# Where a matmul's moving columns come from: one run of memory, or two places in turn

## The chip, the cores and the metric

The kernel runs on one core of a Trainium2 chip. A core has a matmul engine (PE, with its weight loads shown apart as PEld), a vector engine (DVE), a scalar engine (ACT), GpSimd (POOL) and a queue engine that issues most DMAs (SP). Operands lie in an on-chip memory of 128 partitions; matmuls write to a second one, PSUM, from which DVE and ACT read. The metric is the device time of one execution in microseconds (us), the median of several runs.

A matmul has two operands. The *stationary* one, 128 x 128, is loaded into the array by a weight load (LDWEIGHTS); the *moving* one, 128 partitions x 256 or 512 columns, is then streamed through it column by column. Here most operands are of the type fp32r: four bytes a value, rounded, done in one pass. A plain fp32 matmul is done in two.

## The reference

One layer of a trunk with three branches, for 256 tokens of width 2048. All weights are fp32.

```python
h = rms_norm(x, pre_g)
proj = h @ w_in                                  # 2048 -> 7*1024 + 3*2048
a_u, a_v, a_g, b_x, b_g, x_q, x_g, gate_logits = jnp.split(proj, splits, axis=-1)
y_a = spatial_gating(a_u, a_v, sg_ln_g, sg_ln_b, sg_w, sg_b) * jax.nn.silu(a_g)
y_b = s5_branch(b_x, ..., glu_w, glu_b) * jax.nn.silu(b_g)
y_x = memory_cross_attention(x_q, rms_norm(mem, mem_g), xa_wk, xa_wv) * jax.nn.silu(x_g)
branch = jnp.einsum('bsnc,ncd->bsnd', jnp.stack([y_a, y_b, y_x], axis=2), w_branch)
gates = jax.nn.sigmoid(gate_logits.reshape(bsz, seq, N_BRANCH, D_MODEL))
out = jnp.sum(gates * branch, axis=2) @ w_out
return x + rms_norm(out, post_g)
```

The attention reads 256 memory tokens; `s5_branch` is a scan over the 256 positions with a product with `glu_w` behind it.

## The kernel before

**Two halves of every number.** To come close to fp32 with one-pass matmuls, each weight and each activation is split into a high part, rounded to fp32r by ACT, and a low part, the rest, made by DVE (`split`, `split_to`, lines 93 and 94). A product is then high x high + low x high + high x low.

**Two kinds of product.** `cm` products put out channels on the partitions and tokens along the columns: a 128 x 128 block of weights is stationary and the activations move. `cm_mm` does a step over 128 input channels in two matmuls: the high weights against the high and low halves of the activations side by side (512 columns, line 132), and the low weights against the high half (256 columns, line 131, or 134 in the first step). The two sums that stand apart in PSUM are added by `fold` or `fold_u`. `tm` products put out tokens on the partitions: a block of activations is stationary and 512 columns of weights move; `tm_mm` does a step in three matmuls of 512 columns (lines 137 to 139). The normalised x lies in `xhl`, 16 tiles `x` of 128 channels x (high, low) x 256 tokens; the memory tokens lie alike in four tiles `H`, as `mhl`.

**Weights** come from HBM in pieces of 1 MB (`load`, tiles `raw`, three buffers), and are split in halves of 1024 columns into tiles `hl` (three buffers). The host lays them out beforehand (`layouts`: `cm`, `tm`).

**Stages, in PE's order.** The first half of the S5 input (`start`, with x arriving alongside), the rest of it (`w_bx`), queries (`w_xq`), keys (`wk`) and values (`wv`) of the memory, the attention's gate (`w_xg`), then `merge` for the attention branch (`w_gate`, `w_br`), the gating branch (`w_av`, `w_ag`, `w_au`), its merge, the S5 gate (`w_bg`) and its merge with the product by `glu`, and the output (`w_out`, and `w_out3` in two blocks of 256 columns).

**What sets the order.** PE's instructions stand in the order in which the code writes them. Small work (the S5 scan `s5_main`, attention, layer norm, transposes) is made of generators that `pump` advances between the blocks, a few steps at a time, by credits. Splits of weights are issued ahead of it. DVE, ACT and POOL take their instructions in the scheduler's order.

**Names that the change touches.** `norm_split` writes x and the memory tokens as high and low parts. `bc` is the row of 1/rms by token. `s5_prep` splits a block of `u` (the S5 input, later its output) into `uhl` and copies pieces of it to `U4`, which moves in `bu_mm` (line 511). `s5_gelu` works on `u` in place; its split goes to `yg` in the tiles `H2` and `H3`. `evac_k` takes the keys out of PSUM into `kT` (a tile `M`). `attn` uses pieces of the queries `qT` as stationary (line 661) and transposes the weights of attention `p`; `attn_out` writes the attention's output; `sg_z` multiplies by `zT`. `yB` is the S5 branch's output, stationary in the last branch product.

Of the kernel before, what the change touches and what calls it, by code (L numbers as in the profile page):

```python
# [18 lines left out]
P = 128  # L19
# [25 lines left out]
def trunk(ctx: ExitStack, tc: tile.TileContext, I, out):  # L45
# [74 lines left out]

    def norm_split(src, gv, dst, k0):
        for k in range(len(dst)):
            kk = k0 + k
            r = src[:, k * T:(k + 1) * T]
            a.activation(out=dst[k][:, 0], in_=r, func=AF.Copy, scale=gv[:, kk:kk + 1])
            v.scalar_tensor_tensor(out=dst[k][:, 1], in0=r, scalar=gv[:, kk:kk + 1],
                                   in1=dst[k][:, 0].bitcast(F32), op0=ALU.mult, op1=ALU.subtract)

    def cm_mm(ps, wh, wl, hl, first, last):
        if not first:  # L130
            pe.matmul(ps[:, 0:T], lhsT=wl, rhs=hl[:, 0], start=False, stop=False)  # L131
        pe.matmul(ps, lhsT=wh, rhs=hl.rearrange("p h t -> p (h t)"), start=first, stop=last)  # L132
        if first:
            pe.matmul(ps[:, 0:T], lhsT=wl, rhs=hl[:, 0], start=False, stop=False)  # L134

    def tm_mm(ps, wh, wl, hl, ts_, first, last):
        pe.matmul(ps, lhsT=hl[:, 0, ts_], rhs=wh, start=first, stop=False)  # L137
        pe.matmul(ps, lhsT=hl[:, 0, ts_], rhs=wl, start=False, stop=False)  # L138
        pe.matmul(ps, lhsT=hl[:, 1, ts_], rhs=wh, start=False, stop=last)  # L139
# [27 lines left out]
    def cm_block(ps, raw, hl):  # L167
        for hf in range(2):
            wh, wl = split(raw[:, hf * 1024:(hf + 1) * 1024], CM_OFF)
            for k in range(8):  # L170
                kk = hf * 8 + k
                cm_mm(ps, wh[:, k * P:(k + 1) * P], wl[:, k * P:(k + 1) * P], hl[kk], kk == 0, kk == 15)
            pump(rate["cm"])

    def tm_quarter(acc, raw, hl, kq, nk):
        for hf in range(2):
            wh, wl = split(raw[:, hf * 1024:(hf + 1) * 1024])
            for k in range(2):
                kk = kq * 4 + hf * 2 + k
                sl = slice(k * 512, (k + 1) * 512)  # L180
                for tb in range(2):
                    tm_mm(acc[tb], wh[:, sl], wl[:, sl], hl[kk], slice(tb * P, (tb + 1) * P), kk == 0, kk == nk - 1)
# [8 lines left out]
    def cm_pairs(src, nblk, hl, evac):  # L191
        for bp in range(nblk // 2):
            ps = acc_tile()
            for b in range(2):
                cm_block(ps[:, b], load(src[2 * bp + b]), hl)
# [8 lines left out]
    xhl = [xp.tile([P, 2, T], F32R, name=f"x{k}") for k in range(16)]  # L204
# [40 lines left out]
    def rms_row(key, sss, targets):  # L245
# [24 lines left out]
        a.copy(out=bc[:, 0, :], in_=ps[:, 0:T])  # L270
# [13 lines left out]
    mh = [slot(f"H{i}", [P, 4, 2, T], F32R) for i in range(4)]  # L284
    mhl = [mh[k // 4][:, k % 4] for k in range(16)]
# [180 lines left out]
    def s5_load(q):  # L466
        rw = s5p.tile([P, 2, P], F32, tag="rw", name=nm("sb"))
        if q < 2:
            g.tensor_copy(out=rw[:, 0, 0:1], in_=mhl[0][:, 0, 0:1].bitcast(F32))
# [3 lines left out]
    def s5_prep(q, rw, hl):  # L473
# [601 lines left out]
```

## Time and profile before

| | |
|---|---|
| median of 3 runs | 964.48 us (964.4 to 964.81) |
| profiled execution | 964.42 us |
| its span, first to last instruction | 962.7 us |
| DMA engines' mean rate | 201 GB/s |
| weight loads on PE | 4864 |

The profile is one execution. *Busy* is the time in which an engine had an instruction running; for PE the end of a matmul is modelled, and neighbours overlap, so its busy share says that matmuls stood behind each other, not how fast they went. The groups (one line of code, one engine, one shape) give count, busy time, mean duration and idle time before. The order of time gives the start of each instruction. The stage rows give, for a stretch of the span, each engine's busy time, the granted clock of PE and the DMAs' share.

### The profile page before, as it was taken

How to read it: one execution, taken by the hardware profiler on the slowest of the kernel's cores; microseconds unless marked ns; L12 is line 12 of the kernel's file. 1: busy time of each engine (PE TensorE's matmuls, PEld its weight loads, DVE VectorE, ACT ScalarE, POOL GpSimd, SP SyncE). 2: the span in 40 equal slices, each digit the busy share in tenths (PEclk: the TensorE clock that was granted, in tenths of full speed). 3: DMA queues.
4: the chain of work that ended last, by engine and by line, in shares of the span. 5: the costliest groups of instructions: out<-in, count | busy, mean ns of one | idle time of the engine just before them, and what ended most of it. 6: DMA issues, size and time to landing. Idle time of an engine off the chain costs nothing.

```text
span 962.7 us, 13036 instructions
## 1 busy us (share of the span) xinstructions
PE 949.8 (99%) x4864; PEld 799.7 (83%) x4864; DVE 781.2 (81%) x1382; ACT 544.5 (57%) x892; POOL 23.9 (2%) x46
## 2 busy tenths in 40 slices
PE   9999999999999999999999999999999999999996
PEld 7878888888888878888888888888887878888886
DVE  6889759965769989999777799999998966775555
ACT  7555756655456657564544566566656546544442
POOL 1100000000000001000000000000000000000000
PEclk9999999999999999999999999999999999999999
DMA  9757855545355556555555545556555555557542
GB/s 358 257 219 264 303 182 186 212 156 206 131 188 178 207 203 221 201 187 206 181 189 182 203 170 197 186 189 222 180 186 189 196 198 204 182 184 268 198 175 88
DMA packets 30464, 193.34 MB, mean 201 GB/s; under 512 B 3904, under 2 KB 4416, under 8 KB 8640
## 3 DMA queue, kind: packets, MB, share of 16 engines
q1 hardware_dynamic: 28288, 186.18, 54.0%
q0 software_dynamic: 1536, 4.20, 1.2%
q10 hardware_dynamic: 576, 2.12, 0.7%
q8 instruction: 38, 0.62, 0.3%
q14 instruction: 26, 0.21, 0.1%
HBM read 190.39 MB, written 2.10 MB: 200 GB/s over the span
## 4 chain that ended last, share of the span: by engine, by line
PE 88%; DVE 8%; ACT 1%; issue 1%; DMA 1%; POOL 0%; SPq 0%; DVEq 0%; ACTq 0%
PE acc L132 19%; PE acc L137 18%; PE acc L138 18%; PE acc L139 18%; PE acc L131 9%; DVE hl L94 3%; DVE p L323 1%; PE y L576 1%; PE po L692 1%; PE bu L511 1%; ACT hl L93 1%; DMA sb<-s5b 1%; PE acc L134 1%; PE sc L661 1%; DVE p L552 1%
## 5 line engine op out<-in xcount | busy, mean ns | idle before, releaser
L94 DVE TENSOR_TENSOR hl<-raw,hl 128x1024 fp32r<-128x1024 f32 x319 | 388.9, 1219 | 138.6 <-ACT hl L93 137.2
L93 ACT CAST hl<-raw 128x1024 fp32r<-128x1024 f32 x319 | 334.6, 1049 | 269.8 <-PE acc L139 153.2
L132 PE MATMUL acc<-x,hl 128*128 128x512 f32 x736 | 255.6, 393 | 0.5 <-ACT hl L93 0.5
L131 PE MATMUL acc<-x,hl 128*128 128x256 f32 x690 | 194.7, 282 | 1.4 <-DVE hl L94 1.3
L137 PE MATMUL acc<-hl,x 128*128 128x512 f32 x448 | 176.2, 393 | 0.0
L138 PE MATMUL acc<-hl,x 128*128 128x512 f32 x448 | 174.7, 390 | 0.0
L139 PE MATMUL acc<-hl,x 128*128 128x512 f32 x448 | 174.3, 389 | 0.0
L132 PEld LDWEIGHTS acc<-x,hl 128*128 128x128 f32 x736 | 135.9, 188 | 28.2 <-ACT hl L93 1.0
L131 PEld LDWEIGHTS acc<-x,hl 128*128 128x128 f32 x690 | 129.9, 188 | 5.0 <-DVE hl L94 3.0
L137 PEld LDWEIGHTS acc<-hl,x 128*128 128x128 f32 x448 | 84.1, 188 | 18.8 <-issue 2.1
L139 PEld LDWEIGHTS acc<-hl,x 128*128 128x128 f32 x448 | 84.1, 188 | 17.8
L138 PEld LDWEIGHTS acc<-hl,x 128*128 128x128 f32 x448 | 84.2, 188 | 16.6
L137 PE MATMUL acc<-hl,H 128*128 128x512 f32 (+1 forms) x224 | 85.9, 384 | 0.0
L138 PE MATMUL acc<-hl,H 128*128 128x512 f32 (+1 forms) x224 | 85.6, 382 | 0.0
L139 PE MATMUL acc<-hl,H 128*128 128x512 f32 (+1 forms) x224 | 85.5, 382 | 0.0
L132 PE MATMUL acc<-H,hl 128*128 128x512 f32 x192 | 66.4, 394 | 0.3 <-DVE H L94 0.3
L131 PE MATMUL acc<-H,hl 128*128 128x256 f32 x176 | 49.4, 280 | 0.8 <-ACT H L93 0.8
L139 PEld LDWEIGHTS acc<-hl,H 128*128 128x128 f32 x224 | 42.1, 188 | 8.3
L499 ACT ACTIVATE t<-E,pwr 128x32 f32<-128x32 f32 (+2 forms) x96 | 33.9, 354 | 26.6 <-DVE E L326 25.5
L137 PEld LDWEIGHTS acc<-hl,H 128*128 128x128 f32 x224 | 42.1, 188 | 8.2 <-issue 0.4
L138 PEld LDWEIGHTS acc<-hl,H 128*128 128x128 f32 x224 | 42.1, 188 | 7.7
L323 DVE TENSOR_TENSOR p<-p,E 128x512 f32<-128x512 f32 x64 | 44.0, 687 | 0.9
(243 smaller groups left out, 1180.6 us busy)
## 6 DMA issues: line engine op xcount, KB each, us to landing
raw<-w_gate SPq DMA_DIRECT2D x48, 1024.0 KB, 4.7
raw<-w_br SPq DMA_DIRECT2D x24, 1024.0 KB, 4.7
raw<-w_out SPq DMA_DIRECT2D x16, 1024.0 KB, 4.7
raw<-w_xq SPq DMA_DIRECT2D x8, 1024.0 KB, 4.8
raw<-wk SPq DMA_DIRECT2D x8, 1024.0 KB, 4.8
raw<-wv SPq DMA_DIRECT2D x8, 1024.0 KB, 4.9
raw<-w_xg SPq DMA_DIRECT2D x8, 1024.0 KB, 4.7
raw<-w_av SPq DMA_DIRECT2D x8, 1024.0 KB, 4.8
```

The costliest lines, as they stand in the source:

```text
L93: a.copy(out=hi, in_=src)
L94: v.tensor_tensor(out=lo, in0=src, in1=hi.bitcast(F32), op=ALU.subtract)
L131: pe.matmul(ps[:, 0:T], lhsT=wl, rhs=hl[:, 0], start=False, stop=False)
L132: pe.matmul(ps, lhsT=wh, rhs=hl.rearrange("p h t -> p (h t)"), start=first, stop=last)
L134: pe.matmul(ps[:, 0:T], lhsT=wl, rhs=hl[:, 0], start=False, stop=False)
L137: pe.matmul(ps, lhsT=hl[:, 0, ts_], rhs=wh, start=first, stop=False)
L138: pe.matmul(ps, lhsT=hl[:, 0, ts_], rhs=wl, start=False, stop=False)
L139: pe.matmul(ps, lhsT=hl[:, 1, ts_], rhs=wh, start=False, stop=last)
L323: v.tensor_tensor(out=o, in0=i0, in1=i1, op=op)
L499: a.activation(out=t, in_=E[:, :, lo_], func=AF.Copy, scale=ci)
L511: pe.matmul(bu[:, ri, :], lhsT=B4[:, ri, :], rhs=U4, start=True, stop=True)
L552: v.tensor_tensor_scan(out=p2[:, ri], data0=rb, data1=p1[:, ri], initial=0.0, op0=ALU.mult, op1=ALU.add)
```

## The change

Every fp32r matmul takes the columns of its moving operand in turn from two places: first place, second place, first place again one column on. `two` writes that as an access pattern. For a 512-column operand the places are 1 KB apart (256 values); for the 256-column weights of `w_out3` and for `U4` they are half of that.

The data is laid out so that this gives what it gave before:

- The host stores each 512-column block of `tm` weights (and each 256-column block of `w_out3`) with its even columns first and its odd ones behind; taking turns puts them in order again.
- A tile of x or of the memory tokens is now (token half, high or low, 128 tokens), so that tokens b and 128 + b are 1 KB apart (`Pairs`). A `cm` product then puts out its columns as tokens 0, 128, 1, 129 and so on.
- Whatever reads such columns undoes it or keeps to it: `in_order` and `in_order2` read or write them with a step of two (the row of 1/rms, gelu, the attention's output, the gating product), `qT` and `p` give their pieces as every second column, `yB` gives its stationary pieces as every second column (`Plain` with `turn`), and the S5 split undoes two turns at once with a step of four.

Two further edits: the key products use `cm_mm3`, three matmuls of 256 columns that add into one place in PSUM, so that `evac_k` only copies; and the split of the gelu output goes in eight pieces of 256 in place of four of 512.

```diff
+    def two(z):
+        return z.rearrange("p (a b) -> p b a", a=2)
+    def in_order(z):
+        return z.rearrange("p (b c) -> p c b", c=2)
...
+    class Pairs:
...
+        def half(self, h):
+            return self.t[:, :, h]
+        def moving(self, h):
+            return self.t[:, :, h].rearrange("p c b -> p b c")
+        def moving_both(self):
+            return two(self.t.rearrange("p c h b -> p (c h b)"))
+        def stationary(self, h, tb):
+            return self.t[:, tb, h]
+    class Plain:
...
+        def stationary(self, h, tb):
+            return self.t[:, h, tb::2] if self.turn else self.t[:, h, tb * P:(tb + 1) * P]
...
     def cm_mm(ps, wh, wl, hl, first, last):
         if not first:
-            pe.matmul(ps[:, 0:T], lhsT=wl, rhs=hl[:, 0], start=False, stop=False)
-        pe.matmul(ps, lhsT=wh, rhs=hl.rearrange("p h t -> p (h t)"), start=first, stop=last)
+            pe.matmul(ps[:, 0:T], lhsT=wl, rhs=hl.moving(0), start=False, stop=False)
+        pe.matmul(ps, lhsT=wh, rhs=hl.moving_both(), start=first, stop=last)
...
+    def cm_mm3(ps, wh, wl, hl, first, last):
+        pe.matmul(ps[:, 0:T], lhsT=wh, rhs=hl.moving(0), start=first, stop=False)
+        pe.matmul(ps[:, 0:T], lhsT=wh, rhs=hl.moving(1), start=False, stop=False)
+        pe.matmul(ps[:, 0:T], lhsT=wl, rhs=hl.moving(0), start=False, stop=last)
+
+    def tm_mm(ps, wh, wl, hl, tb, first, last):
+        pe.matmul(ps, lhsT=hl.stationary(0, tb), rhs=two(wh), start=first, stop=False)
+        pe.matmul(ps, lhsT=hl.stationary(0, tb), rhs=two(wl), start=False, stop=False)
+        pe.matmul(ps, lhsT=hl.stationary(1, tb), rhs=two(wh), start=False, stop=last)
...
-    xhl = [xp.tile([P, 2, T], F32R, name=f"x{k}") for k in range(16)]
+    xhl = [Pairs(xp.tile([P, 2, 2, P], F32R, name=f"x{k}")) for k in range(16)]
...
-            split_to(hl[:, 0], hl[:, 1], u[:, q // 4, :])
+            split_to(*(hl[:, z].rearrange("p (a c b) -> p a c b", a=2, c=2) for z in range(2)),
+                     u[:, q // 4, :].rearrange("p (b a c) -> p a c b", a=2, c=2))
...
-            pe.matmul(bu[:, ri, :], lhsT=B4[:, ri, :], rhs=U4, start=True, stop=True)
+            pe.matmul(bu[:, ri, :], lhsT=B4[:, ri, :], rhs=two(U4), start=True, stop=True)
...
-        for k in range(4):
-            d = yg[k // 2][:, 2 * (k % 2):2 * (k % 2) + 2]
-            split_to(d[:, :, 0], d[:, :, 1], u[:, 2 * k:2 * k + 2, :])
-            yield 0.7
...
+        for k in range(8):
+            d = nrm["yg"][k]
+            split_to(d.half(0), d.half(1), in_order(u[:, k, :]))
+            yield 0.35
...
     def s5_gelu(cb, ps):
-        y = u[:, cb, :]
-        stt(y, y, d_s5[:, cb:cb + 1], ps, ALU.mult, ALU.add)
+        y = in_order(u[:, cb, :])
+        stt(y, y, d_s5[:, cb:cb + 1], ps.rearrange("p (c b) -> p c b", c=2), ALU.mult, ALU.add)
...
     def evac_k(bp, ps):
-        fold_u(kT[:, 2 * bp:2 * bp + 2, :], ps)
+        a.copy(out=kT[:, 2 * bp:2 * bp + 2, :], in_=ps[:, :, 0:T])
...
-    cm_pairs(I["wk"], 8, mhl, evac_k)
+    cm_pairs(I["wk"], 8, mhl, evac_k, cm_mm3)
...
-                pe.matmul(sc[:, qb, :], lhsT=qT[:, 2 * h + c, qb * P:(qb + 1) * P], rhs=kT[:, 2 * h + c, :],
+                pe.matmul(sc[:, qb, :], lhsT=qT[:, 2 * h + c, qb::2], rhs=kT[:, 2 * h + c, :],
...
-        return np.ascontiguousarray(w.reshape(kq, 4, 128, nn, 512).transpose(3, 0, 2, 1, 4).reshape(nn, kq, 128, 2048))
+        return np.ascontiguousarray(
+            w.reshape(kq, 4, 128, nn, 256, 2).transpose(3, 0, 2, 1, 5, 4).reshape(nn, kq, 128, 2048))
```

Apart from those two edits no instruction is added or taken away, and PE's order is the old one. The first place where it differs is PE at the end of the query products and the start of the key products (`x` and `H` are the moving tiles, `hl` the weights). Before:

```order
L131 MATMUL acc_919<-x_125,hl_983 128x256
L132 MATMUL acc_919<-x_125,hl_983 128x512
L132 MATMUL acc_1013<-H_22_357,hl_1016 128x512
L134 MATMUL acc_1013<-H_22_357,hl_1016 128x256
L131 MATMUL acc_1013<-H_22_357,hl_1016 128x256
```

Now:

```order
L171 MATMUL acc_919<-x_125,hl_983 128x256
L172 MATMUL acc_919<-x_125,hl_983 128x512
L177 MATMUL acc_1013<-H_22_357,hl_1016 128x256
L178 MATMUL acc_1013<-H_22_357,hl_1016 128x256
L179 MATMUL acc_1013<-H_22_357,hl_1016 128x256
```

The first step over 128 channels of the keys was a 512 and a 256; it is three of 256 now, and so are the 127 behind it. The second place is DVE in the key stage (`M_81` is the keys' tile, `U` the S5 input, `X_39` the queries, `bc_x` the row of 1/rms). Before:

```order
L94 TENSOR_TENSOR hl_1197<-raw_1195,hl_1197 128x1024
L295 TENSOR_TENSOR M_81_1011<-acc_1013,M_81_1011 128x512
L282 TENSOR_TENSOR U_126<-U_126,bc_x 128x512 x4
L94 TENSOR_TENSOR hl_1221<-raw_1195,hl_1221 128x1024
L282 TENSOR_TENSOR X_39_542<-X_39_542,bc_x 128x512 x2
L94 TENSOR_TENSOR hl_1254<-raw_1252,hl_1254 128x1024
```

Now:

```order
L94 TENSOR_TENSOR hl_1244<-raw_1242,hl_1244 128x1024
L327 TENSOR_TENSOR U_126<-U_126,bc_x 128x512 x4
L327 TENSOR_TENSOR X_39_542<-X_39_542,bc_x 128x512
L94 TENSOR_TENSOR hl_1276<-raw_1242,hl_1276 128x1024
L327 TENSOR_TENSOR X_39_542<-X_39_542,bc_x 128x512 x2
L94 TENSOR_TENSOR hl_1316<-raw_1314,hl_1316 128x1024
```

The addition into the keys' tile (L295), one of four, is gone, and one scaling of the queries has moved a row up, ahead of a split of weights. The third place is ACT near the end of the S5 work, where the gelu output is split (`H_978` is a tile of `yg`, `gl` and `E` belong to the S5 scan). Before:

```order
L599 ACTIVATE gl_6177<-gl_6177 128x256
L506 ACTIVATE E_6058<-E_6058 128x128 x2
L499 ACTIVATE t_6286<-E_6282,pwr 128x2x16
L93 CAST H_978_7210<-U_126 128x2x256
L93 CAST hl_6184<-raw_6182 128x1024
```

Now:

```order
L645 ACTIVATE gl_6301<-gl_6301 128x256
L552 ACTIVATE E_6182<-E_6182 128x128 x2
L545 ACTIVATE t_6410<-E_6406,pwr 128x2x16
L93 CAST H_978_7334<-U_126 128x2x128
L93 CAST hl_6308<-raw_6306 128x1024
```

One cast of 512 values became two of 256; the other of the pair stands twelve rows earlier.

More of the change, by code (lines that the diff above doesn't have):

```diff
@@ L165, in trunk, with cm_block @@
     rate = {"cm": 0.62, "tm": RT[6]}
-    def cm_block(ps, raw, hl):
+    def cm_block(ps, raw, hl, mm_=cm_mm):
         for hf in range(2):
@@ L282, in mul_to @@
         v.tensor_tensor(out=dst, in0=t, in1=bc, op=ALU.mult)
-    mh = [slot(f"H{i}", [P, 4, 2, T], F32R) for i in range(4)]
-    mhl = [mh[k // 4][:, k % 4] for k in range(16)]
+    mh = [slot(f"H{i}", [P, 4, 2, 2, P], F32R) for i in range(4)]
+    mhl = [Pairs(mh[k // 4][:, k % 4]) for k in range(16)]
     def mem_half(hf):
@@ L716, in hls @@
     def hls(tiles):
-        return [tiles[k // 4][:, k % 4] for k in range(8)]
+        return [Plain(tiles[k // 4][:, k % 4]) for k in range(8)]
     def merge(n, yhl, sink):
@@ L866, in trunk @@
             split_to(d[:, 0], d[:, 1], t[:, i])
+    yBs = [Plain(d, True) for d in yB]
     mm = {}
@@ L898, in trunk @@
         bg[2].append(merge_t(c))
-    mhl2 = [mm_tile(k // 4)[:, k % 4] for k in range(16)]
+    mhl2 = [Plain(mm_tile(k // 4)[:, k % 4]) for k in range(16)]
     gpost = s5c.tile([P, 1, D], F32, tag="cb", name="gpost")
```

57 lines of the change are left out of this document (31 added, 26 removed).

## The prediction

> **What bounds the kernel now.** I read the page first, then the waits of PE, then the order of time of PE in one undisturbed stretch of each kind of product.
>
> ```profile
> span 962.7 us, 13036 instructions
> PE 949.8 (99%) x4864; PEld 799.7 (83%) x4864; DVE 781.2 (81%) x1382; ACT 544.5 (57%) x892; POOL 23.9 (2%) x46
> PE 88%; DVE 8%; ACT 1%; issue 1%; DMA 1%; POOL 0%; SPq 0%; DVEq 0%; ACTq 0%
> ```
>
> PE is busy in 99% of the span and carries 88% of the chain that ended last. In PE's own list of waits the two longest entries are these:
>
> ```profile
> PE wps L202 <- POOL wz L199: 1.4, 1, 1.4
> PE acc L131 <- DVE hl L94: 1.3, 3, 0.7
> ```
>
> So PE hardly ever waits for anybody: the time is its 4864 matmuls, one behind the other. A busy row does not tell how fast each goes (its mean duration has a modelled end), so the step from start to start is what counts. First a stretch of the 512-column products of `tm_mm` (19 starts, the first and the last shown), then one of the 256-column products of the last output block (33 starts):
>
> ```profile
> 299.70 0.39 PE L139 MATMUL acc<-hl,x 128*128 128x512 f32 x1
> ...
> 303.78 0.39 PE L139 MATMUL acc<-hl,x 128*128 128x512 f32 x1
> ```
>
> ```profile
> 944.82 0.28 PE L137 MATMUL oacc<-hl,H 128*128 128x256 f32 x1
> ...
> 948.65 0.28 PE L139 MATMUL oacc<-hl,X 128*128 128x256 f32 x1
> ```
>
> 4.08 us over 18 steps is 226.7 ns for 512 columns; 3.83 us over 32 steps is 119.7 ns for 256. Two points give a line: (226.7 - 119.7)/256 = 0.418 ns a column, and 13 ns for every matmul whatever its width. `cm_mm`'s alternating 512 and 256 fit it too:
>
> ```profile
> 115.40 0.39 PE L132 MATMUL acc<-H,hl 128*128 128x512 f32 x1
> ...
> 116.80 0.39 PE L132 MATMUL acc<-H,hl 128*128 128x512 f32 x1
> ```
>
> Four pairs in 1.40 us are 350 ns a pair; 768 columns at 0.418 are 321 ns, so 29 ns are left for two matmuls. The granted clock is 1.00 throughout (the stage table below), so the columns cannot go faster; only the 13 ns can.
>
> The only matmuls on PE without that loss are the attention scores, in plain fp32. The code has 16 of them and the trace 32 records: each is done in two passes of 256 columns.
>
> ```profile
> 190.60 1.89 PE L661 MATMUL sc<-M,X 128*128 128x256 f32 x8
> 192.14 0.47 PE L131 MATMUL acc<-x,hl 128*128 128x256 f32 x1
> 192.45 0.39 PE L132 MATMUL acc<-x,hl 128*128 128x512 f32 x1
> L661 PEld LDWEIGHTS sc<-M,X x32: 187/190/190, 190.4 to 232.3; 128*128 128x128 f32 x32
> L137 PEld LDWEIGHTS acc<-hl,x x448: 186/188/192, 241.4 to 793.9; 128*128 128x128 f32 x150
> ```
>
> From 190.60 to 192.45 stand eight such records and one 256-column fp32r matmul: (1.85 - 0.12)/8 = 216 ns a record. The line's 0.418 ns is one column for each tick of PE. 512 ticks are 214 ns; a plain record therefore spends two ticks on a column and loses 2 ns, where an fp32r matmul takes a new column every tick and loses 13. The weight loads beside both are alike (190 and 188 ns). So the loss belongs neither to the load alone nor to the end of a matmul, but to a moving operand that must give a new 4-byte column every tick while a load runs.
>
> **The change, part by part.** *The moving operand* (`two`, `Pairs`, the host's `tm`). Each of two places now gives a column every second tick, the pace at which the plain record loses 2 ns. fp32r matmuls: 960 + 896 + 64 in `cm_mm`, 3 x 864 in `tm_mm`, 64 in `bu_mm`: 4576, which with 280 plain records and 8 for warming up is the page's 4864. The trace has no matmul with such an operand, so its price is bounded from both sides: 13 ns saved each (nothing lost any more) at best, and at worst each column costs the two ticks of the plain record. I take the plain record's 2 ns, so 11 ns saved: 4576 x 11.1 = **-50.8 us**, all on PE, which has no cover.
>
> *The keys* (`cm_mm3`): 128 steps of 512 + 256 columns become three of 256. The columns are the same; 128 more matmuls at 2 ns are **+0.3 us**; at the present 13 ns they would be +1.7 us. Four additions on DVE go:
>
> ```profile
> L295 DVE TENSOR_TENSOR M<-acc,M 128x512 f32<-128x512 f32 x4 | 2.7, 683 | 0.0
> 97.80:142.80 45.00, 45.00 (x262) 39.61 (x261) 31.45 (x51) 26.96 (x42) 0.20 (x1) 1.00 0.67 242
> ```
>
> (The second row is that stage; its columns are below.) They are worth 2.7 us where DVE is busy 31 of 45 us: nothing.
>
> *What pays for the new order* on ACT and DVE: reads or writes in steps of 8 or 16 bytes in the U splits, gelu, the attention output and the gating. Element counts are the same, so I take 0. Were the strided side to cost a second pass, the S5 part would pay most: 8 x (474 + 3 x 418) ns = 14 us on DVE, and the 683 to 692 ns rows of the other groups (four each) about 11 more; of these 25 us only what falls in the tight stages below would show, 10 us or so.
>
> ```profile
> L326 DVE SCALAR_TENSOR_TENSOR U<-U,vecs,y 128x256 f32<-128x256 f32 x8 | 3.8, 474 | 1.4 <-PE y L576 1.4
> L323 DVE TENSOR_TENSOR U<-U,gl 128x256 f32<-128x256 f32 x8 | 3.3, 418 | 0.5 <-ACT gl L599 0.5
> L94 DVE TENSOR_TENSOR uhl<-U,uhl 128x256 fp32r<-128x256 f32 x8 | 3.3, 418 | 0.0
> L94 DVE TENSOR_TENSOR H<-U,H 128x512 fp32r<-128x512 f32 x4 | 2.8, 688 | 0.5 <-ACT H L93 0.4
> ```
>
> The split of the gelu output goes from four pieces of 512 to eight of 256: 8 x 418 - 4 x 688 = +0.6 us of DVE, background work in the gated products. No wait, DMA or queue is added or moved.
>
> *Weights in steps of 8 bytes* (`Plain` with `turn`): the 192 loads from `yB` in the last branch product.
>
> ```profile
> L137 PEld LDWEIGHTS acc<-hl,yB x64: 187/188/190, 818.5 to 863.8; 128*128 128x128 f32 x64
> ```
>
> Today 188 ns lie under a step of 227. No load of the trace is strided; I take no change, and were it twice as long it would stick out by 376 - 227 = 149 ns, 29 us in all.
>
> *The next bound.* With PE 5% shorter, DVE is next. The stages where it is busiest, in order `bx`, `w_xq`, `wv`, `w_av`, the first branch's merge, `w_bg`:
>
> ```profile
> core 0: us, PE busy (x) PEld busy (x) DVE busy (x) ACT busy (x) POOL busy (x), PEclk, DMA share, GB/s
> 28.40:50.60 22.20, 22.20 (x129) 19.54 (x128) 19.69 (x72) 11.65 (x19) 2.90 (x4) 1.00 0.72 260
> 50.60:97.80 47.20, 45.94 (x257) 38.98 (x256) 43.49 (x139) 28.50 (x46) 1.06 (x2) 1.00 0.64 239
> 142.80:187.80 45.00, 45.00 (x205) 37.40 (x204) 41.33 (x73) 28.02 (x50) 1.61 (x3) 1.00 0.56 195
> 383.70:429.20 45.50, 45.50 (x215) 37.06 (x214) 43.05 (x77) 28.05 (x51) 2.70 (x4) 1.00 0.58 210
> 521.20:657.60 136.40, 136.40 (x636) 111.81 (x634) 126.02 (x218) 84.40 (x150) 4.83 (x9) 1.00 0.55 192
> 657.60:703.90 46.30, 46.30 (x278) 40.03 (x277) 43.41 (x73) 27.89 (x49) 1.07 (x2) 1.00 0.53 193
> ```
>
> At 11.1 ns for each fp32r matmul (128, 256, 192, 192, 576, 256 of them) PE's stage lengths become 20.8, 44.4, 42.9, 43.4, 130.0 and 43.5 us, against DVE's 19.7, 43.5, 41.3, 43.1, 126.0 and 43.4. DVE is nowhere longer, but in `w_av` and `w_bg` it has no slack left, and a late low half of a weight split makes PE wait. Today at 43.05 of 45.5 us (95%) PE waits for nothing; for six stages at 95 to 100% I put **+4 us**, between 0 and 10. DMA stays hidden: a 1 MB load lands in 4.7 us,
>
> ```profile
> raw<-w_gate SPq DMA_DIRECT2D x48, 1024.0 KB, 4.7
> ```
>
> and its 24 matmuls still take 24 x 216 ns = 5.2 us, with three buffers.
>
> **Sum.** Against the profiled span: 962.7 - 50.8 + 0.3 + 4 = 916.2 us. The profiled run took 964.42, 1.7 us more than its span and as good as the median of 964.48: **918 us**.
>
> **Rivals.** *Half of it.* If the column read and the weight load still meet on part of the ticks (places 512 bytes apart in the 256-wide products of `w_out3` and `bu_mm`, or two streams that meet by chance half as often), half the 50.8 us stays: 962.7 - 25.4 + 1 + 1.7 = 940 us. For it: the loss is spread over all tiles alike, so nothing shows which address matters. Against: the plain record shows the loss nearly gone at half the pace.
>
> *It does not do what it says.* If the 13 ns are the hand-over from one fp32r weight set to the next, the order of the columns is nothing to it. Then only the 128 more matmuls remain: 964.4 + 1.7 = 966 us. For it: the loss is the same at 512 and 256 columns, and each matmul has exactly one load. Against: the plain records swap weights of the same size for 2 ns. The Trainium skill, page TensorE: Matmul & The Clock Gate, section Part 2: What happens when you issue a matmul, says that PE reads the moving operand and the weights through two independent ports, so that loading the next weights takes nothing from the running matmul; that speaks for this rival. The same page, section Back-to-back issue gap, gives N/2.4 + 2.5 ns for a warm matmul, 215.8 ns for 512 columns as an estimate from it; the trace's 226.7 does not agree for fp32r, while its plain records at 216 do.
>
> *Slower: neighbours are lost.* Today consecutive columns are neighbours in memory. If one fetch serves several neighbours, taking turns between two places makes every column a fetch of its own. Its price by the nearest row, the plain record: two ticks a column, 216 ns for 256. The fp32r columns are 3360 x 512 + 1216 x 256 = 2.03 million; another 0.418 ns each are 849 us, so 1813 us in all. It decides from the point where a 512-column step is above 227 ns; a mild form, say one extra tick in fifty, costs 17 us (982). For it: no row shows a strided moving operand at full pace. Against: the plain record shows that half the pace for each place is enough if a place keeps its own fetch. The Trainium skill, page SBUF — State Buffer, section Specifications (TRN2), states just this rule: lines of 16 bytes that need at least two hits each for full bandwidth, with a penalty for each crossing. By it the change would be this rival; no run here shows it yet, since every moving operand of the trace is contiguous.
>
> **How the numbers follow.** Forecast 0.45 (918; by its bounds 904, with no waits and all 13 ns, to 932, with 10 us of waits and strided reads), half 0.20 (940), no effect 0.15 (966), slower 0.20 (982 to 1813). The range holds the first three, 904 to 970, and leaves out 0.20. A difference of 0.2%, 1.9 us, is about the least that a measurement of this kernel can tell from none; 966 lies within it. So faster 0.65, same 0.15, slower 0.20.
>
> **What would show it.** Steps of 216 and 109 ns between starts in undisturbed stretches, the L132 and L137 groups' means down by 11 ns from 393, 256-column ones from 282; PE busy near 900 us; in the waits, PE for DVE's low half (`hl` L94) up from 1.3 to some 4 us, in `w_av` and `w_bg` first. Steps of 227 would be the rival without effect, steps above it the slower one; steps of 216 with a time above 932 would mean that I undervalued DVE.

## The result, and the profile after

| | before | after |
|---|---|---|
| median | 964.47 us (964.4 to 964.81, 4 runs) | 935.77 us (934.47 to 936.64, 4 runs) |
| ratio | | 0.9701, 95% interval 0.9684 to 0.9717 |
| profiled execution, its span | 964.42, 962.7 us | 934.47, 932.7 us |

28.7 us less, or 3.0%. The forecast was 918 us in a range of 904 to 970. The page of the changed kernel, its head and the engines of its chain:

```profile
span 932.7 us, 13296 instructions
PE 912.2 (98%) x4992; PEld 801.5 (86%) x4992; DVE 785.0 (84%) x1382; ACT 544.9 (58%) x896; POOL 22.1 (2%) x46
...
PE 49%; DVE 37%; ACT 7%; issue 5%; DMA 1%; DVEq 0%; POOL 0%; ACTq 0%; POOLq 0%
```

PE has 128 more matmuls and 37.6 us less busy time. The chain that ended last runs through DVE for 37% of the span (8% before): DVE is the second bound now. The order of time on PE, first the 512-column products, then the 256-column ones of the last block, then the key products with `cm_mm3`:

```profile
292.81 0.38 PE L184 MATMUL acc<-hl,x 128*128 128x512 f32 x1
...
294.11 0.38 PE L184 MATMUL acc<-hl,x 128*128 128x512 f32 x1
...
915.83 0.28 PE L184 MATMUL oacc<-hl,H 128*128 128x256 f32 x1
...
919.18 0.28 PE L184 MATMUL oacc<-hl,X 128*128 128x256 f32 x1
...
104.80 0.28 PE L177 MATMUL acc<-H,hl 128*128 128x256 f32 x1
...
106.47 0.28 PE L177 MATMUL acc<-H,hl 128*128 128x256 f32 x1
```

Six steps in 1.30 us are 217 ns for 512 columns (227 before); 30 steps in 3.35 us are 112 ns for 256 (120 before); the keys' 15 steps in 1.67 us are 111 ns. So what a matmul loses beside its columns fell from 13 ns to 3 ns at 512 columns and 5 ns at 256. `cm_mm`'s pairs of 256 and 512 columns take 327 ns (348 before). Adding up what each step from one fp32r matmul to the next has above its columns at 2.4 columns a nanosecond, steps that are less than 60 ns above them lose 62.4 us before and 15.2 us after: 47.2 us are gone. Longer steps, most of them waits, add up to 10.1 us before and 25.9 us after: 15.8 us came back. (That makes 31.4 us, where the span fell by 30.0; the steps to and from other matmuls are not in this count.) What PE waited for, and below it the longest entry for the weight loads:

```profile
PE acc L183 <- DVE hl L94: 4.4, 9, 1.7
PE tp L728 <- DVE p L722: 2.5, 1, 2.5
PE acc L171 <- DVE hl L94: 2.4, 6, 0.7
...
PEld acc L183 <- DVE hl L94: 16.2, 35, 2.0
```

L183 is the second matmul of a `tm` step, the first one that uses the low half of the weights. PE's idle time shows only part of such a wait, because the end of the matmul before is modelled; its weight load waited 35 times, 16.2 us in all. In the kernel before, the loads' longest entry for DVE was 3.0 us, on L131, and the list has none on a `tm` product. One such wait of the changed kernel, in the gating branch's merge, by order of time (PE's sequence cut to three rows around it, with two of their loads and the split that it waited for):

```profile
628.40 1.20 DVE L94 TENSOR_TENSOR hl<-raw,hl 128x1024 fp32r<-128x1024 f32 x1
...
628.85 0.38 PE L182 MATMUL acc<-hl,H 128*128 128x512 f32 x1
...
629.52 0.68 DVE L598 TENSOR_TENSOR_SCAN p<-s5r,p 128x256 f32<-128x256 f32 x1
...
629.66 0.19 PEld L183 LDWEIGHTS acc<-hl,H 128*128 128x128 f32 x1 [0.83 <-DVE hl L94]
629.66 0.48 PE L183 MATMUL acc<-hl,H 128*128 128x512 f32 x1 [0.43 <-DVE hl L94]
629.76 0.19 PEld L184 LDWEIGHTS acc<-hl,H 128*128 128x128 f32 x1
629.98 0.38 PE L184 MATMUL acc<-hl,H 128*128 128x512 f32 x1
```

The split ends at 629.60 and the matmul starts at 629.66. From 628.85 that is 810 ns in place of 216, 0.6 us lost where the profile puts 0.43 down; and the step behind it takes 320 ns in place of 216, because the weight load behind the held one has been held too: it starts at 629.76, 0.10 us after the held matmul, where it elsewhere starts with it. Forty steps of the trace are such second steps, 105 to 108 ns longer.

Where it happens, by stage (`bx`, `w_xq`, `wv`, `w_av`, the gating branch's merge, `w_bg`, the S5 gates; columns as before):

```profile
27.10:48.00 20.90, 20.90 (x129) 19.26 (x128) 19.27 (x71) 13.22 (x22) 1.59 (x4) 1.00 0.76 272
48.00:92.40 44.40, 43.03 (x257) 38.22 (x257) 43.21 (x139) 26.14 (x43) 1.06 (x2) 1.00 0.68 252
136.80:180.50 43.70, 43.31 (x207) 37.55 (x206) 39.92 (x70) 26.66 (x48) 1.61 (x3) 1.00 0.55 187
371.60:417.20 45.60, 43.87 (x216) 37.27 (x214) 44.10 (x79) 27.97 (x53) 2.27 (x4) 1.00 0.59 209
505.60:640.10 134.50, 133.08 (x635) 111.50 (x635) 126.43 (x219) 85.00 (x153) 4.82 (x9) 1.00 0.55 191
640.10:685.80 45.70, 44.89 (x277) 39.28 (x277) 43.11 (x72) 27.83 (x49) 1.07 (x2) 1.00 0.56 203
685.80:774.10 88.30, 87.53 (x427) 73.85 (x426) 77.64 (x127) 49.75 (x81) 0.54 (x1) 1.00 0.56 200
```

`bx` and `w_xq` reached the forecast 20.8 and 44.4 us, `w_xq` with DVE busy 97% of it. `w_av` took 45.6 us, as long as before, with DVE busy 97% of it too: 44.1 us, more than the 43.4 that PE needs there. The merge took 134.5 in place of 130.0, `w_bg` 45.7 in place of 43.5.

The new order was not free on DVE. The U split, which now reads in steps of 16 bytes, went from 418 ns (shown in the prediction) to 808, and the attention output, in steps of 8 bytes, from 683 to 878. After, and the second row before:

```profile
L94 DVE TENSOR_TENSOR uhl<-U,uhl 128x256 fp32r<-128x256 f32 x8 | 6.5, 808 | 0.0
L745 DVE TENSOR_TENSOR H<-po,H 128x512 f32<-128x512 f32 x4 | 3.5, 878 | 0.0
...
L698 DVE TENSOR_TENSOR H<-po,H 128x512 f32<-128x512 f32 x4 | 2.7, 683 | 0.0
```

With gelu (474 to 566, 418 to 517 and 490) and the other rows in steps of 8 bytes (692 to 823 and 820), seven groups grew by some 7 us together.

### The profile page after: what moved, and what is told of

It reads as the page before. It is cut to its first block, busy times and chain, and to the rows that moved or that the text cites. A ratio compares the mean times of both kernels' runs of the same rounds, so it can differ in the third digit from the quotient of the medians.

```text
span 932.7 us, 13296 instructions
## 1 busy us (share of the span) xinstructions
PE 912.2 (98%) x4992; PEld 801.5 (86%) x4992; DVE 785.0 (84%) x1382; ACT 544.9 (58%) x896; POOL 22.1 (2%) x46
## 4 chain that ended last, share of the span: by engine, by line
PE 49%; DVE 37%; ACT 7%; issue 5%; DMA 1%; DVEq 0%; POOL 0%; ACTq 0%; POOLq 0%
DVE hl L94 15%; PE acc L172 11%; PE acc L183 9%; PE acc L184 9%; PE acc L182 9%; DVE p L368 7%; PE acc L171 5%; DVE p L598 4%; ACT hl L93 3%; DVE E L371 2%; DVE s L368 1%; DVE B L528 1%; PE po L738 1%; ACT U L531 1%; DMA raw<-mem 1%
## 5 line engine op out<-in xcount | busy, mean ns | idle before, releaser
L172 PE MATMUL acc<-x,hl 128*128 128x512 f32 x736 | 242.7, 384 | 0.0
L171 PE MATMUL acc<-x,hl 128*128 128x256 f32 x690 | 190.5, 276 | 2.4 <-DVE hl L94 2.4
L183 PE MATMUL acc<-hl,x 128*128 128x512 f32 x448 | 172.4, 385 | 3.9 <-DVE hl L94 3.4
L182 PE MATMUL acc<-hl,x 128*128 128x512 f32 x448 | 171.4, 383 | 0.0
L184 PE MATMUL acc<-hl,x 128*128 128x512 f32 x448 | 169.9, 379 | 0.0
L172 PEld LDWEIGHTS acc<-x,hl 128*128 128x128 f32 x736 | 137.5, 190 | 17.7 <-ACT hl L93 0.7
L171 PEld LDWEIGHTS acc<-x,hl 128*128 128x128 f32 x690 | 132.3, 192 | 6.3 <-DVE hl L94 5.0
L183 PEld LDWEIGHTS acc<-hl,x 128*128 128x128 f32 x448 | 84.8, 189 | 22.6 <-DVE hl L94 11.7
L184 PEld LDWEIGHTS acc<-hl,x 128*128 128x128 f32 x448 | 84.8, 189 | 11.1
L183 PE MATMUL acc<-hl,H 128*128 128x512 f32 (+1 forms) x224 | 84.2, 376 | 1.1 <-DVE hl L94 1.1
L182 PE MATMUL acc<-hl,H 128*128 128x512 f32 (+1 forms) x224 | 83.6, 373 | 0.0
L184 PE MATMUL acc<-hl,H 128*128 128x512 f32 (+1 forms) x224 | 83.3, 372 | 0.0
L183 PEld LDWEIGHTS acc<-hl,H 128*128 128x128 f32 x224 | 42.4, 189 | 8.9 <-DVE hl L94 3.6
L598 DVE TENSOR_TENSOR_SCAN p<-s5r,p 128x256 f32<-128x256 f32 x64 | 43.1, 696 | 0.8
L368 DVE TENSOR_TENSOR p<-bu,E 128x512 f32<-128x512 f32 x64 | 41.8, 685 | 2.0 <-PE bu L557 2.0
```

What stands on the lines that cost most here:

```text
L171: pe.matmul(ps[:, 0:T], lhsT=wl, rhs=hl.moving(0), start=False, stop=False)
L172: pe.matmul(ps, lhsT=wh, rhs=hl.moving_both(), start=first, stop=last)
L182: pe.matmul(ps, lhsT=hl.stationary(0, tb), rhs=two(wh), start=first, stop=False)
L183: pe.matmul(ps, lhsT=hl.stationary(0, tb), rhs=two(wl), start=False, stop=False)
L184: pe.matmul(ps, lhsT=hl.stationary(1, tb), rhs=two(wh), start=False, stop=last)
L368: v.tensor_tensor(out=o, in0=i0, in1=i1, op=op)
```

## The experiments

Two questions: what the 13 ns are, and where the rest of the gain went. T is the theory on record: the loss comes from a weight load that meets a stream of a new column every tick, and what is missing of the gain are waits for DVE.

### How far apart must the two places be?

The kernel before, with only `tm_mm`'s access pattern changed, to another distance in each stage:

```diff
+    def turns(z):
+        return z.rearrange("p (g a b) -> p g b a", a=2, b=n)   # n by stage
-        pe.matmul(ps, lhsT=hl[:, 0, ts_], rhs=wh, start=first, stop=False)
+        pe.matmul(ps, lhsT=hl[:, 0, ts_], rhs=turns(wh), start=first, stop=False)
```

> The kernel before; only tm_mm's moving operand is read in another order (its 512 columns come out permuted, so the output is not the reference's). The two places are 8 bytes apart in wv, 16 bytes in the attention branch's gates, 32 in its branch product, 64 in w_av, 128 in the gating branch's gates, 256 in its branch product, 512 in the S5 branch's gates, 1 KB in its branch product; w_out stays in one run. Theory T (it is enough that each place gives a column every second tick): 216 ns from start to start at every distance, 227 in w_out. Rival D (the distance selects something, as 1 KB in the change's name has it): 216 at 1 KB and 512 bytes, 227 at the small ones. Rival L (columns of one 16-byte group count as one place): 227 at 8 bytes, 216 from 16 bytes on.

Median steps, from start to start, of 512 columns (in the kernel before, each of these stages has a median of 227):

| distance | 8 bytes | 16 | 32 | 64 | 128 | 256 | 512 | 1 KB | one run |
|---|---|---|---|---|---|---|---|---|---|
| ns | 227 | 216 | 216 | 216 | 216 | 216 | 216 | 216 | 227 |

In the profile's groups of two windows of this kernel, in `wv` (8 bytes) and in the first gates (16 bytes), the mean duration, which keeps the same modelled end, differs by the same 11 ns:

```profile
L150 PE MATMUL acc<-hl,H 128*128 128x512 f32 x50 | 19.5, 390 | 0.0
...
L150 PE MATMUL acc<-hl,x 128*128 128x512 f32 x29 | 11.0, 379 | 0.0
```

Rival L was right, T and D were not: 16 bytes are enough, 8 are not. The 1 KB of the change is no condition, and a pattern in two places is not enough by itself.

### Turns of more columns, more places, plain strides

The same, with other patterns:

```diff
+        if kind == "turn":
+            return z.rearrange("p (a g m) -> p g a m", a=2, m=n)
+        return z.rearrange("p (a b) -> p b a", a=n)
```

> The kernel before; only tm_mm's moving operand is read in another order (columns come out permuted). wv: turns of 2 columns between places 1 KB apart; the attention branch's gates: turns of 4; its branch product: turns of 16; the S5 branch's product: turns of 64. w_av: four places 512 bytes apart, one column each; gating branch's gates: 256 places, that is steps of 8 bytes; its branch product: steps of 16 bytes; the S5 gates: 32 places 64 bytes apart; w_out: 64 places 32 bytes apart. Theory T (a place must not be asked every tick): 216 ns with one column a turn and with four places, 227 for turns of 4 and more, since a place is then asked in consecutive ticks. Rival S (any step away from a dense run helps or hurts by itself): steps of 8 and 16 bytes stand apart from four places. If lost neighbours cost a fetch each, steps of 16 bytes and more show 427 ns.

| pattern | median step, ns |
|---|---|
| turns of 2 columns between two places | 334 |
| turns of 4 | 254 |
| turns of 16 | 240 |
| turns of 64 | 227 |
| four places 512 bytes apart | 283 |
| steps of 8 bytes (256 places) | 452 |
| steps of 16 bytes | 461 |
| steps of 32 bytes | 431 |
| steps of 64 bytes | 433 |

Order of time, turns of 2 first, then steps of 8 bytes:

```profile
160.25 0.50 PE L150 MATMUL acc<-hl,H 128*128 128x512 f32 x1
160.58 0.50 PE L151 MATMUL acc<-hl,H 128*128 128x512 f32 x1
...
700.10 0.63 PE L151 MATMUL acc<-hl,x 128*128 128x512 f32 x1
700.55 0.63 PE L149 MATMUL acc<-hl,x 128*128 128x512 f32 x1
```

Of the patterns tried, one column from each of exactly two places is the only one that beats the dense run. My expectation for four places and for turns of 4 was wrong. The slower rival's price is real: plain strides take some 430 to 460 ns. With two places each 16 bytes are still used by four columns, every other tick; but that holds alike for turns of 2 (334 ns), and for four places every fourth tick (283 ns), so why only one column each from two places is fast is not shown. The Trainium skill, page SBUF — State Buffer, section Specifications (TRN2), asks for two hits on a 16-byte line for full bandwidth and puts a price on each crossing. That does not agree with the moving operand here: steps of 8 bytes have two hits a line and take 452 ns, and two places cross at each column and take 216.

### Is it the weight load?

```diff
+        n = P if first or last else MODE[0]      # 64 or 32, by stage
-        pe.matmul(ps, lhsT=hl[:, 0, ts_], rhs=wh, start=first, stop=False)
+        ts_ = slice(ts_.start, ts_.start + n)
+        pe.matmul(ps[0:n], lhsT=hl[:, 0, ts_], rhs=wh, start=first, stop=False)
```

> The kernel before; in the attention branch's and the S5 branch's gates the stationary operand is only the first 64 of 128 columns, in the gating branch's gates and in w_out the first 32, but for the first and the last step of each sum (half or three quarters of those rows of the output are not computed). Theory T (the 13 ns are the weight load meeting the moving reads): the loss shrinks with the load: 220 ns from start to start at 64 columns, 217 at 32, 227 in wv, w_av and the branch products, which stay whole. Rival H (a fixed hand-over at each fp32r matmul): 227 everywhere.

The groups of this kernel by the size of the stationary operand:

```profile
L142 PE MATMUL acc<-hl,x 128*64 128x512 f32 x224 | 88.0, 393 | 0.0
L142 PE MATMUL acc<-hl,H 128*128 128x512 f32 x166 | 64.8, 390 | 0.0
L142 PE MATMUL acc<-hl,x 128*32 128x512 f32 x112 | 44.1, 394 | 0.0
```

The loads did get shorter, from 188 ns to 134 and 108. At 512 columns that saves nothing; the steps are a little longer (medians 230 and 232 ns, against 227). So T's cause falls there: the loss does not grow with the weight load. In the 256-column products of `w_out3`, which this run narrowed to 32 as well, the median step fell from 120 to 114 ns; in narrow products the load may have a part, which stays open. The Trainium skill, page TensorE: Matmul & The Clock Gate, section Part 2: What happens when you issue a matmul, gives the weights a read port of their own. The steps of 512 columns agree with it; those of 256 do not settle it.

### Per matmul or per column, and which bytes count as one place

```diff
+        if MODE[0][0] in ("run_of", "two_of") and wh.shape[1] == 512 and not first and not last:
+            ps, mh_, ml_ = ps[:, 0:n], pick(wh[:, 0:n]), pick(wl[:, 0:n])
-            wh, wl = split(raw[:, hf * 1024:(hf + 1) * 1024])
+            wh, wl = split(raw[:, hf * 1024:(hf + 1) * 1024], MODE[0][2])   # start 0 or 8 bytes past 16
```

> The kernel before; only tm_mm's moving operand changes, in width but for the first and last step of each sum (the columns left out of a step are missing from the output) or in order (columns come out permuted). One run of 448 columns in the S5 branch's gates, 384 in the attention branch's gates, 256 in w_av; two places in turn with 448 in w_out, 384 in the gating branch's gates, 256 in wv. Theory F (13 ns fixed at each matmul, 2.7 with two places): 200.0, 173.3 and 120.0 ns from start to start in one run, 189.4, 162.7 and 112 in two places. Theory C (a price for each column or each 16 bytes): 512 columns lose 13.7, so 448 lose 12.0, 384 lose 10.3 and 256 lose 6.9: 198.6, 170.3 and 113.5 ns. Besides, a test of the 16-byte groups: two places 8 bytes apart, starting 8 bytes into a group, so that each turn crosses to another group (the attention branch's product): 216 ns if aligned groups of 16 bytes are what counts, 227 (as in e1_apart, where each four columns lie in one group) if the distance is; 16 bytes apart with the same start (the S5 branch's product): 216 either way; one run with that start (the gating branch's product): 227.

| columns | one run, ns | above its columns | two places, ns | above its columns |
|---|---|---|---|---|
| 256 | 120 | 13 | 112 | 5 |
| 384 | 173 | 13 | 163 | 3 |
| 448 | 199 to 203 | 12 to 16 | 189 | 2 |
| 512 (e1_apart) | 227 | 13 | 216 | 3 |

Theory F holds: the loss is one of each matmul, not of each column. (In the 448-column run the lowest tenth is at 199 and the median at 203; why it spreads is open.) One run that starts 8 bytes past a boundary took 234 ns, not the 227 expected. With starts 8 bytes past a boundary, distances of 8 and of 16 bytes both gave 227 ns. I had expected 216 and overlooked that in both patterns some columns that follow each other share an aligned group of 16 bytes: columns 2, 6, 3, 7, then 4 takes 7's group.

So a last kernel of this kind set distances and starts apart:

```diff
+            w = 512 // (2 * n) * 2 * n
+            mh_, ml_ = (z[:, 0:w].rearrange("p (g a b) -> p g b a", a=2, b=n) for z in (wh, wl))
```

> The kernel before; only tm_mm's moving operand is read in another order (columns come out permuted, and a few at the end are left out where the distance is not 256). With starts on a 16-byte boundary: two places 16 bytes apart (wv), 1016 bytes apart with 508 columns (the gating branch's gates), 1020 with 510 (its branch product), 1008 with 504 (w_out). With starts 8 bytes past one: 1 KB apart (the attention branch's gates), 32 bytes apart (its branch product). Starts 4 bytes past: 1 KB apart (the S5 branch's gates). Starts 16 bytes past: one run (w_av) and 1 KB apart (the S5 branch's product). Theory N (consecutive columns must always lie in different 16-byte groups): 216 ns for 512 columns at 1 KB whatever the start, and a loss of 2.7 ns with 508, 510 and 504. Theory B (both places must start on a 16-byte boundary): 227 ns for the starts 8 and 4 bytes past, a loss of 13 ns at distances of 1016 and 1020 bytes, 2.7 at 1008; 216 for starts 16 bytes past. One run: 227 under both.

| distance, start past a 16-byte boundary | step above its columns, ns |
|---|---|
| 16 bytes, 0 | 2.7 |
| 1008, 1016 and 1020 bytes, 0 | 3.0, 2.3 and 2.5 |
| 1 KB, 4 bytes | 3.7 |
| 1 KB, 8 bytes | 1.7 |
| 1 KB, 16 bytes | 2.7 |
| 32 bytes, 8 bytes | 11.7 |
| one run, 16 bytes | 18 (13.7 in its lowest tenth) |

For two places in turn theory N agrees with all of them, and B does not: the loss is small where no two columns that follow each other lie in the same aligned 16 bytes. Beyond two places that is not enough: with four places, and in steps of 16 bytes and more, columns that follow each other never share 16 bytes either, and e2_turns has 283 and 431 to 461 ns. The row of 32 bytes, 8 past, has one such pair in sixteen columns, 32 pairs in a matmul, and loses nearly as much as the dense run with 384. So it is not a price for each pair. What the fixed cost is made of stays open, and so does why a single run that starts 8 or 16 bytes further on lost 18 to 21 ns in place of 13.

### How much do the tm products bring alone?

```diff
+    def two(z):
+        return z.rearrange("p (a b) -> p b a", a=2)
-        pe.matmul(ps, lhsT=hl[:, 0, ts_], rhs=wh, start=first, stop=False)
+        pe.matmul(ps, lhsT=hl[:, 0, ts_], rhs=two(wh), start=first, stop=False)
```

with the host's layout of the change for their weights, and nothing else.

> The kernel before with the tm products alone taking turns (two in tm_mm, and the host's layout of their weights); x, memory tokens, keys and S5 stay as before. Theory T: tm steps 216 ns, cm pairs still 347; in the tm stages it gains what the changed kernel gained there: 1.3 + 4.5 + 0 + 1.9 + 2.6 + 2.3 + 4.9 = 17.5 us, so 947 us. Rival without a limit by DVE: 2592 x 11.1 ns = 28.8 us, 936 us.

947.12 us, ratio 0.9817 (0.9800 to 0.9833). So 17.7 us of the 28.7 are theirs, and about 11 us are left, by difference, for x, the memory tokens, S5 and the keys together. Counted as above, the short steps lose 28.9 us less than in the kernel before (28.8 by the prediction's 11.1 ns each), and 10.4 us come back in longer steps.

### The same DVE work left out of both kernels

```diff
-            for ri in range(2):
-                v.tensor_tensor_scan(out=p2[:, ri], data0=rb, data1=p1[:, ri], initial=0.0, op0=ALU.mult, op1=ALU.add)
```

The kernel before:

> The kernel before without the 64 scans of the S5 branch (42 us of DVE; the branch's states are left unscanned). Theory T (PE alone bounds the kernel before): its time falls only by the waits of PE that stood behind DVE, 0 to 4 us, to 960 to 964 us. Rival (DVE already held the kernel before): more than 10 us less.

The changed kernel:

> The changed kernel without the same 64 scans. Theory T (the 16 us by which the gain fell short of 47 stand in waits for DVE's low halves): most of them go, and the time falls from 935.8 to between 918 and 925 us. Rival (what is missing lies on PE itself, in slower steps or more matmuls): 932 us or more.

Before: 963.89 us, ratio 0.999 (0.998 to 0.9999). After: 917.98 us, ratio to the kernel before 0.9514 (0.9500 to 0.9528), where the change with its scans has 0.9701. The same scans, rows of 42 us on DVE (its busy time fell by 35 and 37 us), were worth 1.1 us to the kernel before and are worth 17.8 us now. The longer steps add up to 10.8 us without them, where the change has 25.9 and the kernel before 10.1: what came back as waits stood behind DVE's scans. The stages `w_av`, the gating branch's merge and `w_bg` of the changed kernel without the scans:

```profile
366.30:409.60 43.30, 43.30 (x216) 37.30 (x215) 40.22 (x72) 28.69 (x53) 2.72 (x4) 1.00 0.64 228
497.40:627.10 129.70, 129.70 (x635) 112.39 (x634) 118.85 (x206) 85.94 (x154) 4.83 (x9) 1.00 0.57 203
627.10:670.70 43.60, 43.60 (x278) 39.44 (x277) 40.43 (x67) 27.95 (x49) 1.07 (x2) 1.00 0.57 203
```

They are the lengths that the prediction worked out for PE alone: 43.4, 130.0 and 43.5 us. The strided rows are still in this kernel, so by themselves they hold up none of the three.

### The keys as before

```diff
-        a.copy(out=kT[:, 2 * bp:2 * bp + 2, :], in_=ps[:, :, 0:T])
+        fold_u(kT[:, 2 * bp:2 * bp + 2, :], ps)
-    cm_pairs(I["wk"], 8, mhl, evac_k, cm_mm3)
+    cm_pairs(I["wk"], 8, mhl, evac_k)
```

> The changed kernel with the key products done as before (512 and 256 columns a step, the low sum folded in by DVE). Theory T: 128 matmuls less at some 5 ns each are 0.6 us on PE, four additions of 0.7 us come back to a DVE with slack: 934 to 936.5 us against 935.8, no difference. Rival (DVE holds the key stage too): 2 to 3 us slower.

934.78 us (933.67 to 935.87), ratio to the kernel before 0.9689 (0.9674 to 0.9703): its interval covers the change's 0.9701, so no difference can be told. That edit of the change is worth at most some 2 us here; it was priced at nothing.

### Giving DVE's work another pace

The background work is dealt out by credits that the change left as they were. `RT` holds them, each for half a piece of weights: for `w_xq`, `wk`, `w_xg`, `w_ag`, `w_au` and `w_bg`, and last for all `tm` stages. First less of it in the tm stages:

```diff
-RT = (0.66, 0.94, 0.47, 0.75, 0.38, 0.85, 1.36)
+RT = (0.60, 1.00, 0.60, 0.70, 0.55, 0.80, 1.27)
```

> The changed kernel with other credits for the background work: 1.27 in place of 1.36 a half piece in the tm stages, and 0.60, 1.00, 0.60, 0.70, 0.55, 0.80 in place of 0.66, 0.94, 0.47, 0.75, 0.38, 0.85 in the cm ones, so that a split of 1.22 us and the credit fit into 12 steps of 216 ns. Theory T: PE waits less for DVE in w_av, the merges and w_bg, and the time falls to 925 to 931 us. Rival (the waits come from the order of the work, not its amount): within 1 us of 935.8, or slower, where late work piles up before the S5 merge.

935.78 us, ratio 0.9702 (0.9688 to 0.9716): the same as the change. The stages `w_av`, the merge, and the S5 gates show why:

```profile
371.50:414.60 43.10, 43.10 (x215) 37.10 (x214) 41.69 (x73) 27.81 (x49) 2.72 (x4) 1.00 0.64 232
502.40:633.40 131.00, 130.28 (x636) 112.23 (x636) 124.22 (x213) 82.96 (x146) 4.29 (x8) 1.00 0.56 197
678.30:774.10 95.80, 88.53 (x430) 74.77 (x428) 87.73 (x155) 57.79 (x102) 1.61 (x3) 0.98 0.54 191
```

`w_av` and the merge got 2.5 and 3.5 us shorter, as meant, and the S5 gates, where all that is left of the scan must be done, 7.5 us longer, with 10 us more of DVE. So the forecast of 925 to 931 us failed: late work piled up before the S5 merge, as its rival had named. The second pace therefore defers the same but does more earlier, where DVE has room:

```diff
+RT = (0.66, 1.05, 0.85, 0.75, 0.62, 0.82, 1.27)
```

> The changed kernel with other credits for the background work, 1.27 in place of 1.36 a half piece in the tm stages as in e7_after_pace, but with what is deferred there done earlier, where DVE has slack: 1.05, 0.85 and 0.62 in place of 0.94, 0.47 and 0.38 in the keys, the attention's gate and w_au, 0.82 in place of 0.85 in w_bg. Theory T (the amount of DVE work in a stage against PE's length sets the waits): w_av, both merges and w_bg shorten as in e7_after_pace, by 8 us, and the S5 gates stay at 88 us: 926 to 929 us. Rival (the work can't be done earlier, since its generators wait for each other there): the S5 gates lengthen again, 934 us or more.

929.74 us, ratio 0.9635 (0.9622 to 0.9648), 6 us better than the change; a little short of the 926 to 929 expected. The third goes further the same way:

```diff
+RT = (0.66, 1.05, 1.10, 0.75, 0.62, 0.78, 1.22)
```

> The changed kernel with credits of 1.22 a half piece in the tm stages, and 1.05, 1.10, 0.62, 0.78 for the keys, the attention's gate, w_au and w_bg (e10_after_pace2 had 1.27, 1.05, 0.85, 0.62, 0.82). The S5 gates had 10 us of DVE to spare there. Theory T: w_av, the gating branch's merge and w_bg come 3 to 4 us nearer to their lengths in e5_after_noscan, the S5 gates stay within 1 us: 925 to 928 us. Rival (what is deferred lands in the S5 gates): 930 us or more.

927.79 us, ratio 0.9618 (0.9605 to 0.9631), the fastest version of the study that leaves nothing out: 36.8 us or 3.8% below the kernel before, and 8 us below the change. Its stages `w_av`, merge and S5 gates:

```profile
370.60:414.70 44.10, 43.80 (x215) 37.10 (x214) 42.19 (x73) 26.70 (x49) 2.45 (x4) 1.00 0.61 213
503.30:636.20 132.90, 131.21 (x636) 111.95 (x635) 126.22 (x219) 86.04 (x153) 4.29 (x8) 1.00 0.56 198
679.90:766.20 86.30, 86.30 (x428) 74.29 (x426) 77.93 (x128) 51.89 (x84) 1.07 (x2) 1.00 0.59 205
```

The S5 gates have PE busy for all of their 86.3 us, and `w_bg` fell to 43.8 us. The merge is still 3 us from its 129.7: DVE does as much there as in the change, and the larger credit in `w_au` did not bring work forward there (DVE 33.5 us, 37.8 in the change); why stays open.

## Why the prediction was right and wrong

- **PE bounds the kernel before.** Right: 42 us less of DVE gave it 1.1 us.
- **A fixed loss of 13 ns for each fp32r matmul, which two places take away.** Right in size, and fixed it is, from 256 to 512 columns. The steps came to 216 and 112 ns (forecast 216 and 109), and the sum of losses fell by 47.2 us where the prediction had 50.8 - 0.3. Most of the difference lies in the matmuls of 256 columns standing by themselves, which keep some 5 ns, not 2, and in the `cm` pairs, which keep 7 ns, not 4.
- **Why they take it away.** Wrong. The prediction said that the load of the next weights meets the stream, as the plain fp32 records seemed to show. At 512 columns narrower loads save nothing, and two places 8 bytes apart, where each place is also asked only every second tick, keep the loss; what counts for two places is whether consecutive columns share an aligned 16 bytes. The plain records were a good price and a bad explanation, so that the price came out right was in part luck. (Nor are the scores the only such records: the plain fp32 products of the attention's output, L692, step by 216 ns too. And a plain record has 256 columns: its 216 ns stand beside a 512-column step only by counting two ticks for each column.)
- **"+4 us, between 0 and 10" for the next bound.** Mis-sized, and most of the miss: longer steps, those 60 ns or more above their columns, grew by 15.8 us, outside the bounds. That is 11.8 of the 16.5 us by which the span came out longer than forecast; 3.3 are the losses above, the rest lies in steps beside other matmuls. Without the scans the changed kernel runs in 917.98 us, near the forecast's 918, which had counted 4 us of waits. The prediction had named this sign itself: steps of 216 ns with a time above 932 us. (By its own terms that bound is 934: 918, 6 more of waits, 10 for strided reads.) The stage sums were nearly right (DVE at 95 to 100% and nowhere above PE; only in `w_av` did DVE's work grow past PE's, to 44.1 us), but I read "DVE fits" as "DVE hardly waits". Splits of 1.2 us stand in one queue with scans and products of 0.4 to 0.7 us, so a low half can be late before DVE is full: in `w_av`, at 97%, all of the gain was gone, in the merge, at 94%, 4.5 of 6.4 us. The share alone does not decide it: `w_xq` kept its gain at 97%, and so did `w_av` under the first pace, at 97% as well. And a wait of this kind costs a second step, 107 ns, behind it.
- **Keys, strided weights, DMA.** Right at nothing: the keys cannot be told apart, the strided loads from `yB` take 197 ns in place of 188 under steps of 216, and no transfer is among PE's longest waits.
- **Strided reads and writes on DVE, taken as 0.** Wrong on DVE: "element counts are the same" does not carry over to time, and some 7 us came on top, the 16-byte steps at nearly twice the time. As four additions went, DVE's busy time shows only 785.0 us after 781.2. What share of the 15.8 us this has was not separated.
- **The rivals.** "Half of it" gives 940, near the measured 935.8, but for another reason: the loss did go, and part of the time was given back as waits. "Neighbours are lost" did not happen at two places; four places and plain strides are slower, as it had it.

## What to carry to other kernels

When the busiest engine is busy 99% of the span, look at its steps from start to start against the work in them: a line through two sizes splits off a fixed cost that no busy row shows. Before counting a gain on that engine, set the next engine's busy time against the new length of each stage. Where it comes near, as at 94 and 97% here, the gain may come back as waits: two stages lost most or all of it, another at 97% none, so the share is a warning and the late operands in the trace decide. Moving that work is then a second change, worth 8 us here. Work that is deferred must have a place to go before the stage that needs it.

## What the runs showed of the hardware

- An fp32r matmul on this chip took its columns at 2.4 a nanosecond plus a fixed 13 ns with a dense moving operand (256 to 512 columns; 16 to 21 in three of the test stages, unexplained), and plus 2 to 5 ns when one column came from each of two places in turn, from 16 bytes to 1 KB apart, as long as consecutive columns did not share an aligned 16 bytes.
- No other pattern did better than the dense run: turns of 2, 4, 16 and 64 columns took 334, 254, 240 and 227 ns for 512 columns (227 dense), four places 283, steps of 8 to 64 bytes 431 to 461.
- A narrower stationary operand did not shorten a 512-column step: 230 and 232 ns with 64 and 32 columns, 227 with 128. A 256-column step went from 120 to 114 ns with 32.
- On DVE a split of 128 x 256 fp32 values took 418 ns from dense reads and 808 with reads in steps of 16 bytes; elementwise rows in steps of 8 bytes took 11 to 29% longer than dense.
- A matmul held up by a late operand cost the one behind it about 107 ns more, in 40 places of the changed kernel's trace.
